# Laying out weights in advance, modulation by multiply-and-sum into columns, and a beginning by single chunks, in a decoder layer on one core

## The chip, the core and the metric

The kernel runs on one core of one Trainium2 chip. The metric is the device time of one execution in microseconds (us), lower is better. Engines are named as in the profile: PE does matmuls (PEld its weight loads), DVE is the vector engine, ACT the scalar engine, POOL the general one, and SP issues most of the transfers (DMAs). Each engine takes its instructions in the order of its own queue, and waits on semaphores for others.

## The reference

One layer of a decoder, 256 rows (SEQ) of width 2048 (D_MODEL), all in float32. A conditioning vector c gives six modulation vectors of 2048 each; the rest is a normalisation, a large input projection, three kinds of attention, an output projection and a SwiGLU FFN.

```python
mod = jax.nn.silu(c) @ w_ada[l] + b_ada[l]          # w_ada: 2048 x 12288
shift1, scale1, gate1, shift2, scale2, gate2 = jnp.split(mod[:, None, :], N_MOD, axis=-1)
h = rms_norm(x, norm1_gain[l]) * (1 + scale1) + shift1
x = x + gate1 * mixing_sublayer(h, w_in[l], ...)    # w_in: 2048 x 13840
h = rms_norm(x, norm2_gain[l]) * (1 + scale2) + shift2
x = x + gate2 * swiglu(h, w_ffn_in[l], w_ffn_out[l])   # D_FF = 5632
```

Of the 13840 columns of w_in, 16 (from column 7680) are a low-rank gate; the others are taken in blocks of 512.

## The kernel before

**Products.** x is kept turned, features on partitions: `xT` and the modulated `hT` are 16 chunks (k) of 128 features by 256 rows. A product of a block of 512 weight columns is done in three matmuls for each chunk and each of two row tiles (`mm3`, L173 to L176): high by high, low by high, high by low, with each float32 operand split into a high and a low half. The high half of a weight tile is cast by ACT (L166, or L244 in pairs), the low half subtracted by DVE (L167, or L230). `load_weights` brings two chunks of 512 columns a transfer, through SP, into a ring "raw" of 4 tiles. `block` (L178) runs the chunks of a block and calls `tick`, which lets so many steps of background work run per pair of chunks. Where two blocks are done together (`fast_products` and `load_pair`, L217), products of sums and differences of blocks save one in eight; these are the gate columns of the projection, FFN units from 2 on, and the output.

**Order.** The first projection goes through groups of chunks, `GROUPS` = (0,3), (3,7), (7,11), (11,16), so that the product of the first chunks can begin while the modulation of the later ones is still computed. For each group, all 13 first blocks of columns are multiplied by the group's chunks, and the sums stay in slots A0 to A12. A scheduler sorts the instructions by priority and by their order in the program; `prio` raises a stretch of the program by a number of steps, and `issue_after` ties an instruction behind another.

**Modulation.** w_ada is read in rows (k on partitions), and `ada_mac` (L426, L432) multiplies a piece of it by silu(c) of that chunk (`csil`, one value per partition) and adds it to an accumulator of as many columns: 16 pieces per accumulator. What is left then is a sum over the partitions. For columns, `turn_acc` has PE transpose the accumulator, 128 columns at a time (L481), and DVE sums the turned tile (L486, L1123); `finish_columns` adds the bias b_ada. For rows spread over all partitions (gate1, gate2), `rows_of` and `rows_of_gate2` multiply the accumulator's halves by a matrix of ones on PE (L1144, L1145, L1620). The first group's accumulator is built from 16 pieces of 128x768 before any product; norm1 is computed from x in rows, which PE turns with a diagonal matrix; `keep_warm` (L590) issues matmuls without use in PE's idle time. The accumulator of shift1 and scale1 lives in slot "ada", and so, in turn, does that of shift2 and of scale2. 24 of the 32 pieces of gate2 are taken in the output projection w_out and FFN units 0 and 1, the other 8 in the output stage (`gate2_end`).

**FFN.** Units 0 and 1 of 11 are done one block at a time, gate columns, then up columns; DVE multiplies the two (L1555). Before unit 2 the program drains all background work (`flush`). From unit 2 on, `load_pair` loads into a ring of the 4 "raw" tiles and `MORE_RAWS`: slot "AR1" until unit 10 and slot "ada" until unit 9. Unit 2's first load goes to "ada".

```python
    MORE_RAWS = (("AR1", 10), ("ada", 9))
    state["raws"] = state["tiles"] = 0
    for i in range(NFF):
        if i == FAST[0]:
            flush()
        state["more_rooms"], state["more_raws"] = rooms_until(i, MORE_ROOMS), rooms_until(i, MORE_RAWS)
```

## Time and profile before

| what | value |
|---|---|
| median of 3 runs | 1574.76 us (1573.27 to 1574.9) |
| profiled execution's span | 1573.4 us, 20259 instructions |
| matmuls of L174, L175, L176 into acc from whi, wlo and H | 998 each, mean 390 to 393 ns |
| low halves of single loads, L167 on DVE | 277, 323.0 us |
| multiply-and-adds of 128x1024 into "ada" from ring AR, L432 on DVE | 39, 49.8 us, mean 1282 ns |
| DMA | 402.26 MB, mean 256 GB/s |

The span is that of one execution taken by the profiler, and stands 1.4 us below the median of the timed runs. A matmul's duration in the trace overlaps its neighbours', so its cost on PE is read from the distance of two starts. The rows of a timeline are: start, duration, engine, line, operation, output <- inputs, shapes, count, and in brackets the idle time before it with what ended it. A name such as `ada<-w_ffn_in` means a transfer or an instruction that writes the tile in slot "ada" from w_ffn_in.

### The profile page before, as it was taken

The page shows a single profiled execution, that of the slowest core. Times are in us where ns is not written, and L with a number is a line of the kernel's source. Part 1 is how long each engine was busy: PE and PEld are TensorE (multiplying, and loading weights), DVE is VectorE, ACT ScalarE, POOL GpSimd, SP SyncE. Part 2 cuts the span into 40 slices and gives each one's busy share as a digit, 9 for nine tenths or more (in the row PEclk, how much of TensorE's full clock was granted, in tenths as well). Part 3 has the DMA queues.
Part 4 walks back from the last instruction along what each step waited for, and adds up shares of the span by engine and source line. Part 5 has one row for each costly group of instructions (what it writes and reads, how often), then busy time and mean ns, then how long its engine had stood idle before and what let it go on. Part 6 is the DMA issues. An engine that isn't in the chain of part 4 may idle for free.

```text
span 1573.4 us, 20259 instructions
## 1 busy us (share of the span) xinstructions
PE 1563.8 (99%) x7180; PEld 1294.6 (82%) x7180; DVE 1404.4 (89%) x1722; ACT 879.7 (56%) x1220; POOL 12.4 (1%) x24
## 2 busy tenths in 40 slices
PE   9999999999999999999999999999999999999998
PEld 7878888888888888888888888888888888888887
DVE  6889996898898999987987889999999999899996
ACT  5654448875765555444444645556555555455553
POOL 1000000000000000000000000000000000000000
PEclk9999999999999999999999999999999999999999
DMA  9999997677797877989997896665666567876664
GB/s 333 355 326 319 335 316 232 217 223 227 238 320 261 275 258 238 314 278 324 313 331 263 298 310 218 191 210 189 202 210 203 174 200 236 289 229 201 222 213 135
DMA packets 196317, 402.26 MB, mean 256 GB/s; under 512 B 13102, under 2 KB 28116, under 8 KB 196216
## 3 DMA queue, kind: packets, MB, share of 16 engines
q1 hardware_dynamic: 194952, 397.75, 76.4%
q0 software_dynamic: 1088, 3.16, 0.5%
q8 instruction: 56, 0.92, 0.2%
q14 instruction: 45, 0.37, 0.1%
q10 hardware_dynamic: 176, 0.07, 0.0%
HBM read 395.68 MB, written 5.24 MB: 255 GB/s over the span
## 4 chain that ended last, share of the span: by engine, by line
PE 94%; ACT 2%; DVE 2%; DMA 1%; issue 1%; ACTq 0%; DVEq 0%
PE acc L176 21%; PE acc L174 21%; PE acc L175 21%; PE misc L176 8%; PE misc L174 8%; PE misc L175 8%; PE acc L590 1%; PE misc L959 1%; ACT whi L166 1%; PE misc L1310 1%; DVE wlo L167 0%; PE misc L583 0%; DMA AR<-w_ada 0%; PE misc L481 0%; DMA raw<-w_in 0%
## 5 line engine op out<-in xcount | busy, mean ns | idle before, releaser
L166 ACT CAST whi<-raw 128x1024 fp32r<-128x1024 f32 (+1 forms) x277 | 278.9, 1012 | 285.9 <-PE acc L176 174.7
L167 DVE TENSOR_TENSOR wlo<-raw,whi 128x1024 fp32r<-128x1024 f32 (+1 forms) x277 | 323.0, 1176 | 98.0 <-ACT whi L166 96.9
L174 PE MATMUL acc<-whi,H 128*128 128x512 f32 x998 | 390.9, 393 | 0.9 <-ACT H L602 0.8
L175 PE MATMUL acc<-wlo,H 128*128 128x512 f32 x998 | 389.7, 390 | 0.7 <-DVE wlo L167 0.7
L176 PE MATMUL acc<-whi,H 128*128 128x512 f32 x998 | 389.7, 391 | 0.5 <-DVE H L609 0.4
L176 PEld LDWEIGHTS acc<-whi,H 128*128 128x128 f32 x998 | 187.6, 188 | 40.9 <-DVE H L609 1.7
L174 PEld LDWEIGHTS acc<-whi,H 128*128 128x128 f32 x998 | 187.7, 188 | 39.2 <-ACT H L602 1.0
L175 PEld LDWEIGHTS acc<-wlo,H 128*128 128x128 f32 x998 | 187.8, 188 | 38.8 <-DVE wlo L167 1.1
L244 ACT CAST whi<-raw 128x1024 fp32r<-128x1024 f32 (+1 forms) x126 | 121.0, 973 | 69.0 <-PE acc L176 28.4
L230 DVE TENSOR_TENSOR wlo<-raw,whi 128x1024 fp32r<-128x1024 f32 (+1 forms) x126 | 139.9, 1124 | 12.8 <-ACT whi L244 11.5
L176 PE MATMUL acc<-whi,A 128*128 128x512 f32 x221 | 86.0, 389 | 0.0
L174 PE MATMUL acc<-whi,A 128*128 128x512 f32 x210 | 82.0, 390 | 0.0
L175 PE MATMUL acc<-wlo,A 128*128 128x512 f32 x210 | 81.7, 389 | 0.0
L174 PE MATMUL misc<-whi,H 128*128 128x512 f32 (+1 forms) x185 | 71.6, 387 | 0.0
L176 PE MATMUL misc<-whi,H 128*128 128x512 f32 (+1 forms) x185 | 71.6, 387 | 0.0
L175 PE MATMUL misc<-wlo,H 128*128 128x512 f32 (+1 forms) x185 | 71.5, 387 | 0.0
L230 DVE TENSOR_TENSOR A<-raw,A 128x1024 fp32r<-128x1024 f32 (+2 forms) x58 | 55.6, 964 | 0.5
L432 DVE SCALAR_TENSOR_TENSOR ada<-AR,csil,ada 128x1024 f32<-128x1024 f32 x39 | 49.8, 1282 | 4.2 <-DMA AR<-w_ada 4.2
L176 PEld LDWEIGHTS acc<-whi,A 128*128 128x128 f32 x221 | 41.5, 188 | 8.7
L244 ACT CAST A<-raw 128x1024 fp32r<-128x1024 f32 (+1 forms) x35 | 34.5, 991 | 25.0 <-PE acc L176 14.8
L244 ACT CAST whi<-A 128x1024 fp32r<-128x1024 f32 x26 | 27.4, 1056 | 36.0 <-DVE A L230 28.1
L175 PEld LDWEIGHTS acc<-wlo,A 128*128 128x128 f32 x210 | 39.4, 188 | 8.1
(710 smaller groups left out, 3078.3 us busy)
## 6 DMA issues: line engine op xcount, KB each, us to landing
raw<-w_in SPq DMA_DIRECT2D x190, 512.0 KB, 4.9
raw<-w_ffn_in SPq DMA_DIRECT2D x135, 512.0 KB, 4.7
raw<-w_ffn_out SPq DMA_DIRECT2D x73, 512.0 KB, 5.0
AR<-w_ada SPq DMA_DIRECT2D x61, 512.0 KB, 4.6
raw<-w_out SPq DMA_DIRECT2D x32, 512.0 KB, 5.9
OS<-w_ada SPq DMA_DIRECT2D x24, 512.0 KB, 5.9
AR<-w_ffn_in SPq DMA_DIRECT2D x22, 512.0 KB, 4.3
KD<-w_ada SPq DMA_DIRECT2D x21, 512.0 KB, 5.1
```

The source lines that it names most:

```text
L166: state["cast"] = nc.scalar.copy(hi[:, :n, :], raw[:, :n, :])
L167: state["split"] = nc.vector.tensor_tensor(lo[:, :n, :], raw[:, :n, :], hi[:, :n, :].bitcast(F32), op=ALU.subtract)
L174: nc.tensor.matmul(ps, lh, rh, start=start, stop=False, skip_group_check=seeded)
L175: nc.tensor.matmul(ps, lh, rl, start=False, stop=False, skip_group_check=seeded)
L176: state["mm"] = nc.tensor.matmul(ps, ll, rh, start=False, stop=stop, skip_group_check=seeded)
L230: done = nc.vector.tensor_tensor(dst, x, y, op=ALU.subtract)
L244: nc.scalar.copy(hi[:, :n, :], src)
L432: nc.vector.scalar_tensor_tensor(acc, raw, c, acc, op0=ALU.mult, op1=ALU.add)
L590: state["warm"] = nc.tensor.matmul(ps, ones_r, wide, start=True, stop=True)
L959: nc.tensor.matmul(ps[:n, t * N_GLA + h, :].rearrange("p (s l) -> p s l", l=L), at(f, h, t)[:, :n], odd(at(f, h, t)), start=True, stop=True,)
L1310: nc.tensor.transpose(ps[:, i, :], src[:, i * P : (i + 1) * P], ident)
```

## The change

**Layout in numpy.** Every weight matrix is laid out as blocks [column block, 128 partitions, chunk, 512], so that a load of two chunks reads 4 KB in one piece per partition instead of two rows of 2 KB. x comes turned (`x_t`) and in blocks (`x_blocks`), w_ada turned (`ada_t`), all small vectors with c and b_ada as columns of one array (`k_vec`), the 16 gate columns of w_in alone (`w_a`). The loads and turns of vectors go.

**Modulation.** silu(c) is spread once over all partitions, as a row of 2048, in `cB`, which takes slot "ada" and stays there. With w_ada turned, a piece is 128 modulation outputs on partitions by 1024 inputs; `column_mac` multiplies it by half of cB and sums along the row in one instruction, into one column. Two give an output column of 128, the bias being the start value. So there are 192 of them: 64 for shift1 and scale1, 32 each for shift2, gate1, scale2 and gate2. The transposes and sums on PE and DVE go. Rows (silu(c) itself, gate1, gate2) are made by `spread`: halves, one transpose, 16 matmuls of 128x128 with a broadcast column of `pick`, and four copies.

**Beginning.** `first_chunks` takes the first four blocks of columns by single chunks (0, 1, 2) into all eight PSUM banks; norm1 is a multiplication of turned x by a spread root (`normed`); h is made chunk by chunk behind its modulation (`ada_chunks`), not at the end of a group.

**gate2.** All 32 of its pieces are taken in w_out and FFN units 0 and 1, with rates 0.9 and 0.7 there; `gate2_end` goes.

```diff
+    cB = S("ada", [P, D])
+    def column_mac(v, seg, j, half, raw):
+        o = BADA + seg * KC + j
+        part = v[:, 0, j : j + 1]
+        return nc.vector.tensor_tensor_reduce(
+            out=raw, in0=raw, in1=cB[:, half * HALF : (half + 1) * HALF], scale=1.0,
+            scalar=part if half else vec[:, o : o + 1], op0=ALU.mult, op1=ALU.add,
+            accum_out=v[:, 1, j : j + 1] if half else part,
+        )
...
+    def spread(v, quarters, tag, first=False):
+        t = S(tag, [P, 2, P], F32R)
+        hl, vT = t[:, 0, :], t[:, 1, :]
+        nc.vector.memset(hl.bitcast(F32), 0.0)
+        nc.vector.tensor_copy(hl[:, :KC], v)
+        nc.vector.tensor_tensor(hl[:, KC : 2 * KC], v, hl[:, :KC].bitcast(F32), op=ALU.subtract)
...
+            nc.tensor.transpose(ps, hl.bitcast(F32), ident)
+        nc.scalar.copy(vT, ps)
...
+                    state["spread"] = nc.tensor.matmul(
+                        ps[:, j * P : (j + 1) * P], pick[:, k : k + 1].to_broadcast([P, P]), vT, start=True, stop=True
+                    )
+            (nc.vector.tensor_copy if first else nc.scalar.copy)(dst, ps)
...
+    def ada_chunks(k0, k1):
+        for k in range(k0, k1):
+            if k % 4 == 0:
+                normed(state["root"], k, k + 4)
+            for seg in (SEG_SCALE1, SEG_SHIFT1):
+                for half in range(2):
+                    with prio():
+                        raw = S(ADA_TAGS[count % len(ADA_TAGS)], [P, HALF])
+                        load_column(raw, seg, k, half)
...
+                            column_mac(mod1[seg], seg, k, half, raw)
+                    if half and seg == SEG_SHIFT1:
+                        make_h(k)
+                    yield
...
+        for k in range(k1):
+            if k:
+                with tc.issue_after(state["h_lo"].ins):
+                    chunk_macs(k, rows[4 * k : 4 * k + 4])
...
+            for i, b in enumerate(ahead):
+                for t in range(NT):
+                    mm3(pss[i][t], *h_at(k, t), *parts[k][i], k == 0, k == k1 - 1)
...
-RATES_OP, RATES_FFN, RATE_OUT = (0.85, 0.5, 0.0), (0.75, 0.9, 0.7, 0.6), 0.5
+RATES_OP, RATES_FFN = (0.9, 0.7, 0.0), (0.75, 0.9, 0.7, 0.6)
...
-WARM = (22, 38, 13)
+WARM = (5, 4, 3, 3, 3, 18)
...
     def gate2_bg():
-        acc = biased([S(tag, [P, 2 * NB]) for tag in ("OS0", "T3")], SEG_GATE2)
-        yield from ada_segment_steps(acc, SEG_GATE2, None, False, range(GATE2_CUT))
+        yield from ada_segment_steps(gate2_v, SEG_GATE2, None)
         yield from last_macs()
-    def gate2_end():
...
-                state["load"] = nc.sync.dma_start(
-                    raw[:, :n, :],
-                    src[ka * P : (ka + n) * P, c0 : c0 + w].rearrange("(k p) c -> p k c", p=P),
-                )
+                state["load"] = nc.sync.dma_start(raw[:, :n, :], src[b, :, ka : ka + n, :])
...
-    gate_pair(1, GATE_PAIRS_3, misc_bank, acc_bank, (("A9", "A10"), ("X1", "T0"), ("ada",)), ("X2", "A8"))
+    gate_pair(1, GATE_PAIRS_3, misc_bank, acc_bank, (("A9", "A10"), ("X1", "T0"), ("T4", "T5")), ("X2", "A8"))
...
-        xs = S("ada", [P, D])
+        xs = []
+        for tag in ("OS0", "T3"):
+            xs += [x for x in S(tag, [P, 2, NB]).rearrange("p a c -> a p c")]
```

**What stands in the queues.** Rows give the line, the operation, the output and its inputs with their tile numbers, and the shape.

DVE at the beginning, before: the last full multiply-and-adds into the accumulator of group 0, then the last piece in quarters, the bias, and h (H is a half of h).

```order
L432 SCALAR_TENSOR_TENSOR ada_329<-OS_39_166,csil,ada_329 128x768
L432 SCALAR_TENSOR_TENSOR ada_329<-OD_168,csil,ada_329 128x768
L432 SCALAR_TENSOR_TENSOR ada_329<-A_41_170,csil,ada_329 128x2x128 x3
L492 TENSOR_TENSOR mod_101<-misc_348,bada 128x1 x2
L492 TENSOR_TENSOR mod_101<-misc_358,bada 128x1 x2
L495 SCALAR_TENSOR_TENSOR mod_101<-mod_101,vec 128x1 x2
L606 TENSOR_SCALAR scr_354<-T_6_102,mod_101 128x256
```

The same place in the changed kernel, DVE, chunk 1: an ISA row of 128x1024 is a multiply-and-sum, the ISA row of 128x1 behind it reads its sum; L639 is a low half of two blocks' weights.

```order
L423 ISA T_19_111,scale_92<-T_19_111,ada_90,vec 128x1024
L423 ISA scale_92 128x1
L423 ISA A_21_113,shift_91<-A_21_113,ada_90,vec 128x1024
L423 ISA shift_91 128x1
L423 ISA T_20_112,scale_92<-T_20_112,ada_90,scale_92 128x1024
L423 ISA scale_92 128x1
L423 ISA A_22_114,shift_91<-A_22_114,ada_90,shift_91 128x1024
L423 ISA shift_91 128x1
L431 SCALAR_TENSOR_TENSOR scale_92<-scale_92,vec 128x1
L639 TENSOR_TENSOR wlo_312<-raw_136,whi_311 128x1024
L564 TENSOR_SCALAR scr_307<-T_2_93,scale_92,shift_91 128x256
```

Sixteen multiply-and-adds ahead of the first h have become four multiply-and-sums ahead of each chunk's.

DVE between FFN unit 1 and unit 2, before: L1555 are unit 1's products of gate and up; A_1870 is a part of unit 2's pairs, from a tile in "ada".

```order
L1555 TENSOR_TENSOR scr_8394<-scr_8394,acc_8398 128x512
L1555 TENSOR_TENSOR scr_8396<-scr_8396,acc_8399 128x512
L230 TENSOR_TENSOR X_1866_8600<-KD_8586,X_1865_8599 128x1024
L230 TENSOR_TENSOR wlo_8596<-OD_8585,whi_8595 128x1024
L432 SCALAR_TENSOR_TENSOR T_1561_7147<-A_1812_8330,csil,T_1561_7147 128x1024
L230 TENSOR_TENSOR A_1870_8608<-ada_8603,A_1869_8607 128x1024
```

In the changed kernel, DVE at the same place (L1484 are the products, ada_90 is cB, L228 is L230 before):

```order
L1484 TENSOR_TENSOR scr_8135<-scr_8135,acc_8139 128x512
L1484 TENSOR_TENSOR scr_8137<-scr_8137,acc_8140 128x512
L423 ISA KC_8067,gate_6786<-KC_8067,ada_90,gate_6786 128x1024
L423 ISA gate_6786 128x1
L228 TENSOR_TENSOR wlo_8349<-OD_8338,whi_8348 128x1024
...
L423 ISA KD_8232,gate_6786<-KD_8232,ada_90,vec 128x1024
L423 ISA gate_6786 128x1
L228 TENSOR_TENSOR KD_8339<-AR_1795_8332,OD_8338 128x512
L423 ISA KC_8259,gate_6786<-KC_8259,ada_90,gate_6786 128x1024
L423 ISA gate_6786 128x1
```

Seven multiply-and-sums of gate2 stand behind the products (four of them in the rows left out), the last of them the last reader of cB in slot "ada".

SP, before, amid the loads of unit 1 (raw, L152): the first load of unit 2 into "ada".

```order
L152 DMA raw_8072<-w_ffn_in 128x2x512
L531 DMA T_1773_8103<-w_ada 128x1024
L224 DMA ada_8553<-w_ffn_in 128x2x512
L152 DMA raw_8078<-w_ffn_in 128x2x512
```

SP, changed: the load into "ada" stands behind the last load of w_ada's gate2 columns.

```order
L416 DMA KD_8232<-ada_t 128x1024
L416 DMA KC_8259<-ada_t 128x1024
L222 DMA AR_1825_8396<-w_ffn_in 128x1024
L222 DMA ada_8306<-w_ffn_in 128x1024
L222 DMA raw_8394<-w_ffn_in 128x1024
```

PE, changed, at the same place: acc_8140 is the up block of unit 1, misc_8458 the first product of unit 2, A_1783 the high half of the tile in "ada".

```order
L172 MATMUL acc_8140<-whi_8185,H_1600_7365 128x512
L173 MATMUL acc_8140<-wlo_8186,H_1600_7365 128x512
L174 MATMUL acc_8140<-whi_8185,H_1604_7369 128x512
L172 MATMUL misc_8458<-A_1783_8308,H_1597_7362 128x512
L172 MATMUL misc_8459<-A_1783_8308,H_1597_7362 128x512
```

The load of unit 2's first pair has moved from the middle of unit 1's loads to behind gate2's last ones, and unit 2's first product, which needs that pair, follows unit 1's last matmul directly on PE.

More of the change, by code (lines that the diff above doesn't have):

```diff
@@ L39 @@
 AHEAD = 4000
[L40 to L41 removed]
+WARM = (5, 4, 3, 3, 3, 18)
+FIRST = 4
+BADA = 58
 GROUPS = ((0, 3), (3, 7), (7, 11), (11, 16))
@@ L473, in column_sum @@
-    def column_sum(ps, acc):
-        return nc.tensor.matmul(ps, acc, ones[:, 0:1], start=True, stop=True)
-    def turn_acc(acc, behind=None):
-        ps = misc_bank([P, acc.shape[1] // P, P])
-        for i in range(acc.shape[1] // P):
-            with tc.issue_after(behind) if behind is not None else nullcontext():
-                nc.tensor.transpose(ps[:, i, :], acc[:, i * P : (i + 1) * P], ident)
-        return ps
-    def turned_sums(dst, acc, behind=None):
-        nc.vector.reduce_sum(dst, turn_acc(acc, behind), axis=AX.X)
@@ new lines, in squares, with root_of @@
+    def squares(j, sums):
+        sq = S(("X1", "X2", "AR0", "AR1")[j], [P, 4, T])
+        nc.scalar.activation(sq, xT[j], AF.Square)
+        for n in (2, 1):
+            nc.vector.tensor_tensor(sq[:, :n], sq[:, :n], sq[:, n : 2 * n], op=ALU.add)
+        return nc.tensor.matmul(sums, ones, sq[:, 0, :], start=j == 0, stop=j == 3)
+    def root_of(sums):
+        act = nc.scalar.activation
+        v, y, z, r = (x for x in S("X0", [P, 4, T]).rearrange("p a t -> a p t"))
+        act(v, sums, AF.Identity, bias=eps_c[:, 0:1], scale=1.0 / D)
@@ L1129, in rows_of, with columns @@
[L1129 to L1147 removed]
+    def columns(seg, v):
+        if seg == SEG_SCALE2:
+            scaled_gain(v, ROW_N2, 0, KC)
+        mod2[seg] = v[:, 1, :]
+        yield
@@ L1148, in rows_of @@
+    def rows_of(name, v, tags):
+        rows = [S(tag, [P, 2 * NB]) for tag in tags]
+        quarters = [a[:, c : c + NB] for a in rows for c in (0, NB)]
+        yield from spread(v[:, 1, :], quarters, {"gate1": "T6", "gate2": "X0"}[name])
         state[name] = quarters
-    def halves(acc):
-        return [acc[:, : 2 * NB], acc[:, 2 * NB :]]
     def background():
         for seg in (SEG_SHIFT2, SEG_GATE1, SEG_SCALE2):
-            if seg == SEG_GATE1:
-                acc = biased([S(f"T{4 + j}", [P, 2 * NB]) for j in range(2)], seg)
-                yield from ada_segment_steps(acc, seg, rows_of("gate1", seg, acc), False)
-            else:
-                acc = S("ada", [P, D])
-                yield from ada_segment_steps(halves(acc), seg, columns(seg, acc))
+            v = columns_of(f"mod_{seg}")
+            done = rows_of("gate1", v, ("T4", "T5")) if seg == SEG_GATE1 else columns(seg, v)
+            yield from ada_segment_steps(v, seg, done)
@@ L1602, in trunk, with gate2_steps @@
     hooks = {at: (lambda n=n: sums_of_unit(n)) for n, at in enumerate((2, 4, 6))}
[L1603 to L1625 removed]
+    state["rate"] = 0.0
+    gate2_rows = rows_of("gate2", gate2_v, ("A2", "A3"))
+    def gate2_steps(n):
+        for _ in range(n):
+            next(gate2_rows, None)
     for n in range(2):
```

525 lines of the change are left out of this document (206 added, 319 removed).

## The prediction

> **What bounds the kernel now.** I read the page's busy times first, then its chain of work that ended last, then busy times by stretch.
>
> ```profile
> PE 1563.8 (99%) x7180; PEld 1294.6 (82%) x7180; DVE 1404.4 (89%) x1722; ACT 879.7 (56%) x1220; POOL 12.4 (1%) x24
> PE 94%; ACT 2%; DVE 2%; DMA 1%; issue 1%; ACTq 0%; DVEq 0%
> 0.00:32.00 32.00, 29.08 (x150) 24.22 (x150) 19.63 (x36) 15.52 (x35) 4.26 (x13) 1.00 0.96 340
> 32.00:84.00 52.00, 51.69 (x224) 42.46 (x224) 42.86 (x51) 32.15 (x51) 0.00 (x0) 0.97 1.00 350
> 84.00:157.00 73.00, 71.88 (x319) 58.91 (x319) 68.97 (x81) 36.32 (x44) 0.00 (x0) 1.00 0.92 318
> 157.00:239.00 82.00, 82.00 (x368) 67.61 (x367) 79.46 (x108) 38.76 (x47) 0.00 (x0) 1.00 0.95 321
> 951.00:976.00 25.00, 25.00 (x116) 20.77 (x115) 24.47 (x29) 13.14 (x16) 1.06 (x2) 1.00 0.60 202
> 957.52 0.39 PE L176 MATMUL acc<-whi,H 128*128 128x512 f32 x1
> 957.75 0.39 PE L174 MATMUL misc<-A,H 128*128 128x512 f32 x1
> ```
>
> PE is busy 99% and is 94% of the chain, so a matmul taken away is worth its pace. The stretch rows give length, then PE, PEld, DVE, ACT and POOL, the granted clock, the DMA share and GB/s. In the stretch that holds FFN units 1 and 2 (the fifth), PE is busy for all 25.00 us, at one 512-column matmul per 957.75 − 957.52 = 0.23 us; and the step to unit 2 is that pair of rows, with no gap. But DVE stands at 24.47 of 25.00 there and at 79.46 of 82.00 in group 2 of the projection: it is a near second, and whatever the change makes DVE or its buffers do late, PE feels.
>
> **The change, part by part.** The sum is made against this execution's span, 1573.4 us; the median of the runs is 1574.76, so 1.4 is added at the end.
>
> *PE work.*
>
> ```profile
> 82.34 1.04 PE L481 MATMUL misc<-ident,ada 128*128 128x128 f32 x8
> 83.14 0.47 PE L174 MATMUL acc<-whi,H 128*128 128x512 f32 x1
> 682.29 0.28 PE L1144 MATMUL misc<-T,ones_r 128*128 128x256 f32 x1
> 682.53 0.40 PE L174 MATMUL acc<-whi,A 128*128 128x512 f32 x1
> 1442.09 0.39 PE L1620 MATMUL misc<-AR,ones_r 128*128 128x512 f32 x1
> 1442.32 0.39 PE L1620 MATMUL misc<-A,ones_r 128*128 128x512 f32 x1
> 307.32 0.22 PE L850 MATMUL misc<-T,ones_r 128*128 128x128 f32 x1
> 307.38 0.40 PE L849 MATMUL misc<-T,T 128*128 128x384 f32 x1
> ```
>
> Eight transposes of L481 hold PE from 82.34 to 83.14, 0.10 each; 50 go after the beginning: −5.0. The gate1 rows go: 8 pairs of 256 columns at 682.53 − 682.29 = 0.24 a pair, −1.9. The gate2 rows go: 8 at 0.23, −1.85. `spread` brings 2 × 16 matmuls of 128 columns and 2 transposes. One of 128 columns with a plain operand takes 307.38 − 307.32 = 0.06; a broadcast stationary operand is not in the trace, so 0.06 to 0.10 (the transpose's pace), and I take 0.08: +2.6, with the transposes +0.2. Net **−6.0** (−7 to −5). The 512-column products stay at 6,378.
>
> *The price d of one reduce.* The change has 192 multiply-and-reduce instructions of 128x1024, each followed by a 128x1 accumulator read. Neither is in the trace. Nearest rows:
>
> ```profile
> 953.75 1.28 DVE L432 SCALAR_TENSOR_TENSOR OS<-A,csil,OS 128x1024 f32<-128x1024 f32 x1
> 954.94 1.22 DVE L230 TENSOR_TENSOR wlo<-raw,whi 128x1024 fp32r<-128x1024 f32 x1
> 956.08 0.69 DVE L230 TENSOR_TENSOR KD<-AR,OD 128x512 f32<-128x512 f32 x1
> 956.68 0.69 DVE L230 TENSOR_TENSOR wlo<-AR,whi 128x512 fp32r<-128x512 f32 x1
> 0.80 0.06 DVE L342 MEMSET eps_c<- 128x1 f32 x1 [0.80 <-PEq L1678]
> 11.44 0.18 ACT L560 ACTIVATION_READ_ACCUMULATOR H<-A 128x1 f32 x1
> ```
>
> By starts, the multiply-and-add occupies DVE for 1.19, the subtraction of the same size 1.14, one of half the size 0.60. The read lies between 0.06 (a 128x1 memset) and 0.18 (ACT's read). So d is 1.14 + 0.06 = 1.20 to 1.28 + 0.18 = 1.46; I take 1.28, the multiply-and-add's start-to-start plus a short read.
>
> [...]
>
> *The beginning.*
>
> ```profile
> 14.71 1.06 ACT L560 ACTIVATE H<-A 128x1024 f32<-128x1024 f32 x1 [0.23 <-DMA A<-x]
> 32.31 0.65 PE L174 MATMUL acc<-whi,H 128*128 128x512 f32 x1 [0.80 <-ACT H L602]
> 32.76 0.63 PE L175 MATMUL acc<-wlo,H 128*128 128x512 f32 x1
> 35.75 0.47 PE L176 MATMUL acc<-whi,H 128*128 128x512 f32 x1
> 32.33 0.88 DVE L609 TENSOR_TENSOR H<-scr,H 128x256 fp32r<-128x256 f32 x2
> 84.13 0.73 PE L174 MATMUL acc<-whi,H 128*128 128x512 f32 x2
> 85.53 0.50 PE L175 MATMUL acc<-wlo,H 128*128 128x512 f32 x1 [0.67 <-DVE wlo L167]
> 92.12 0.72 PE L176 MATMUL acc<-whi,H 128*128 128x512 f32 x2 [0.40 <-DVE H L609]
> ```
>
> Before, the first product starts at 32.31, after loads of about 3.7 MB that had landed when the last x part was read (14.71) and 16 multiply-and-adds. Afterwards, what chunk 0 needs is about as many bytes (vectors, x, its first three modulation pieces), four reduces and one h: 14.7 + 4 × 1.28 + 0.6 puts the first product near 20.5 (two low halves of h at 32.33 take 0.88). Those 12 us are not all kept, since DVE then paces the stage. A chunk of four blocks costs DVE 4 × 1.28 + 2 × 1.14 + 0.6 = 8.0 and PE 24 × 0.23 = 5.5. DVE ends chunk 2 at about 40.7 (three chunks of 8.0 from 16.7); the nine other blocks need 9 × (1.14 + 0.60) of splits, beside them 16 reduces at 1.28 for group 1, and about 4.7 of normalisation and h: 40.8, to 81.5. PE ends group 0 near 87.3, with the last blocks' matmuls behind their splits. Before, group 1 begins at 84.13 and waits to 85.53, say 85.1 of useful time. **+2** (−1.6 with d at 1.20 to +6 at 1.46). The wait for H near 92 goes with the group-end making of h: **−0.7**. Groups 1 and 2 give DVE 36 reduces in place of 32 multiply-and-adds in pieces; the 97% busy stretch has little room, I put **+1** (0 to 4).
>
> *gate2 and FFN unit 2: the deciding term.* The spread silu(c) sits in slot "ada" until gate2's last reduce. The FFN's first fast unit, unit 2, takes its first weight pair into that same slot. Before, the slot is free there, and the load is issued amid unit 1's loads. Afterwards, the load waits for the last gate2 reduce; seven reduces stand in DVE's queue behind unit 1's products (L1555 before), which wait for PE's last matmul of unit 1. And PE's next matmul needs the cast of that pair. Nothing else stands in PE's queue between them. So PE is idle for the whole chain:
>
> ```profile
> 957.88 1.28 DVE L1555 TENSOR_TENSOR scr<-scr,acc 128x512 f32<-128x512 f32 x2
> 959.09 1.23 DVE L230 TENSOR_TENSOR X<-KD,X 128x1024 fp32r<-128x1024 f32 x1
> ada<-w_ffn_in SPq DMA_DIRECT2D x19, 512.0 KB, 5.3
> gate<-T POOLq DMA_DIRECT2D x1, 512.0 KB, 2.9
> T<-w_ada SPq DMA_DIRECT2D x15, 512.0 KB, 6.7
> L244 ACT CAST A<-ada 128x1024 fp32r<-128x1024 f32 x6 | 6.3, 1051 | 0.7 <-PE misc L176 0.7
> ```
>
> Two products 959.09 − 957.88 = 1.21; seven reduces 8.96; the split and the half-size subtraction that stand among them 1.14 + 0.60; issue to landing 5.3 (the group's median; transfers of this size elsewhere take 2.9 to 6.7); the cast 1.05. Together 11.9 + 5.3 + 1.05 = **18.3** (15.3 with d at 1.20 and the shortest transfer, 20.9 with 1.46 and the longest). The transfer has no neighbours to hide behind: the wait is SP's, and the weights queued behind it on SP are late too, by the same time, not more. After a stop PE may come back slow, as at 32.31, where eight matmuls to 35.75 took 0.43 each: 8 × 0.20 = **+1.6** (0 to 2.9). The gap here is far longer than the 0.80 us wait ahead of that row.
>
> The slots of other tiles that change hands (distances, gate rooms, norm2's rows) keep their sizes, and the warm-up matmuls run while PE waits for the first product: nothing for both, unless a slot's last reader is late, which would show as a wait like the one above.
>
> gate2 itself moves 8 multiply-and-adds from the output stage into w_out and units 0 and 1; PE has no wait on DVE of size in either stage that this would lift, so I put it at nothing. The relayout in numpy leaves bytes and the size of each load as they are.
>
> ```profile
> L166 ACT CAST whi<-raw 128x1024 fp32r<-128x1024 f32 (+1 forms) x277 | 278.9, 1012 | 285.9 <-PE acc L176 174.7
> ```
>
> The casts that read the loads are idle 285.9 us, and 174.7 of it ends with a matmul that frees a buffer, not with a transfer: PE's need for loads is covered, and faster ones are worth nothing where that holds. With the cover gone each load would cost up to its 5 us.
>
> Sum: −6.0 + 2 − 0.7 + 1 + 18.3 + 1.6 = +16.2: a span of 1589.6, a run of **1591**.
>
> **The rivals.** *A, faster.* The load into "ada" is not held: the reduces finish, and the pair lands and is cast, before PE's last matmul of unit 1. Then −6.0 + 2 − 0.7 + 1 = −3.7: 1571. It decides from the point at which the seven reduces stand ahead of unit 1's products on DVE. Against it: their place in the queue, which is fixed by program order. For it: DVE runs ahead of PE elsewhere. If moreover the beginning keeps its 12 us (reduces far cheaper than any row), 1563. Chance 0.09. *B, much slower.* [...] Chance 0.05. *C, no change.* The chain is half hidden (say four reduces already done, a short transfer and a quick clock, 10 us less) and the beginning 4 better: +2, 1577. Chance 0.04.
>
> **How the numbers follow.** Forecast 0.82. All low ends: −7 − 1.6 − 0.7 + 0 + 15.3 + 0 = +6.0, a run of 1581. All high ends: −5 + 6 − 0.7 + 4 + 20.9 + 2.9 = +28.1, 1603. The range 1580 to 1604 holds the forecast and leaves out A, B and C, 0.18. A measurement can tell about 0.2%, 3.1 us, from no change. Faster by more is A (0.09), within it C (0.04), slower the forecast and B (0.87).
>
> **What would show it.** One PE gap of 15 to 21 us between unit 1's last and unit 2's first matmul, released by ACT's cast from "ada", behind a transfer issued right after the last reduce. First product near 20.5; group 0 ended near 87. Rows of L481, L1144 and L1620 gone. A reduce and its read at 1.20 to 1.46 by starts. What would make it wrong: the reduces before the products on DVE, a price far from 1.28, or PE gaps in groups 1 and 2 that DVE's lead does not cover.

## The result, and the profile after

The changed kernel takes 1607.98 us (median of 4 runs, 1606.77 to 1610.35) against 1574.01 us of the kernel before, measured beside it: a ratio of 1.0218, with an interval of 1.0206 to 1.0231. It is 34 us slower. The prediction was 17 us slower, 1591, in a range of 1580 to 1604: the direction and the largest single cause were right, the sum was half of what came.

The page of the changed kernel, the lines that answer to those shown of before:

```profile
span 1608.6 us, 19949 instructions
PE 1556.9 (97%) x7043; PEld 1283.5 (80%) x7043; DVE 1406.2 (87%) x1889; ACT 866.1 (54%) x1185; POOL 4.0 (0%) x11
PE 75%; DVE 10%; DMA 7%; ACT 4%; issue 4%; SPq 0%; DVEq 0%; ACTq 0%
```

PE is busy for 6.9 us less than before (1563.8) and the span is 35 us longer, so PE stands idle for 42 us more. (A part of the busy time that is gone is warm-up: 36 such matmuls in place of 73.) The chain that ended last was PE for 94%, and DVE, DMA and ACT had 5% of it; now these hold 21%, since the chain leaves PE at each long wait and follows a queue back.

The same stretches as before, and the one with the change from FFN unit 1 to unit 2 (columns as before: length, PE, PEld, DVE, ACT, POOL, granted clock, DMA share, GB/s):

```profile
0.00:32.00 32.00, 22.51 (x85) 17.85 (x85) 23.84 (x51) 11.99 (x16) 0.69 (x6) 1.00 0.96 362
32.00:84.00 52.00, 44.94 (x174) 33.89 (x175) 48.23 (x77) 28.59 (x46) 0.00 (x0) 0.93 0.86 299
84.00:157.00 73.00, 73.00 (x321) 59.78 (x320) 67.84 (x93) 37.74 (x45) 0.00 (x0) 1.00 0.93 332
157.00:239.00 82.00, 80.49 (x355) 66.33 (x354) 78.24 (x112) 36.70 (x42) 0.00 (x0) 1.00 0.92 324
960.00:1000.00 40.00, 20.52 (x81) 16.02 (x80) 29.15 (x40) 10.51 (x12) 0.00 (x0) 0.70 0.53 178
```

In the last row PE is busy for half of the time and stands at 0.70 of its clock. In the second PE is busy for 7 us less than before in the same stretch, while DVE has gone from 42.86 to 48.23.

Where PE stands still shows in its timeline: in brackets the idle time and what ended it.

```profile
33.06 1.65 PE L172 MATMUL acc<-whi,H 128*128 128x512 f32 x3 [2.97 <-ACT H L560]
...
68.76 0.73 PE L172 MATMUL acc<-whi,H 128*128 128x512 f32 x2 [0.94 <-ACT whi L164]
70.02 0.50 PE L173 MATMUL acc<-wlo,H 128*128 128x512 f32 x1 [0.52 <-DVE wlo L165]
...
220.12 0.50 PE L173 MATMUL acc<-wlo,H 128*128 128x512 f32 x1 [1.51 <-DVE wlo L165]
...
415.72 0.69 PE L777 MATMUL misc<-ident,A 128*128 128x128 f32 x2 [2.81 <-DVE A L765]
...
586.03 0.50 PE L172 MATMUL acc<-whi,H 128*128 128x512 f32 x1 [1.56 <-ACT whi L242]
587.36 0.50 PE L173 MATMUL acc<-wlo,H 128*128 128x512 f32 x1 [0.83 <-DVE wlo L228]
...
670.61 0.30 PE L367 MATMUL misc<-ident,T 128*128 128x128 f32 x1 [2.24 <-DVE T L359]
...
780.85 0.50 PE L173 MATMUL acc<-wlo,A 128*128 128x512 f32 x1 [1.13 <-DVE wlo L165]
...
988.76 1.22 PE L172 MATMUL misc<-A,H 128*128 128x512 f32 x2 [19.43 <-ACT A L242]
```

The matmuls of `mm3` are 6378 in both kernels (24 of them of 256 columns, the others of 512). Apart from the first four blocks they come in the same order but for a few, so the start of the n-th in one trace can be set beside the n-th of the other. The difference, worked out in this way, is the lag of the changed kernel; it is that of one execution each, and that of the changed kernel was the slowest of its four (1610.35):

| product | where | lag, us |
|---|---|---|
| 0 | first product | −7.9 |
| 100 | in group 0 | +0.9 |
| 260 | group 1 | +2.8 |
| 860 | end of group 2 | +2.5 |
| 1180 | first blocks of the last group | +0.1 |
| 1500 | after the wait at 415 us | +6.4 |
| 2140 | after the waits at 587 us | +8.1 |
| 2500 | after the wait at 670 us | +13.2 |
| 3700 | end of FFN unit 1 | +11.4 |
| 3740 | in unit 2 | +34.4 |
| 6377 | last | +35.1 |

So of 35 us, 23 come at unit 2, 9 between products 860 and 3700, and about 3 in the beginning. In seven small steps of 0.5 to 0.9 us, 5.4 together, the lag shrinks where the transposes of L481 are gone.

The wait at unit 2, by the queues of DVE, SP and ACT:

```profile
970.94 1.28 DVE L1484 TENSOR_TENSOR scr<-scr,acc 128x512 f32<-128x512 f32 x2
972.13 1.28 DVE L423 CUSTOM_DVE_ANT_0 KC<-KC,ada,gate 128x1024 f32<-128x1024 f32 x1
...
979.30 1.28 DVE L423 CUSTOM_DVE_ANT_0 KD<-KD,ada,vec 128x1024 f32<-128x1024 f32 x1
...
981.23 1.28 DVE L423 CUSTOM_DVE_ANT_0 KC<-KC,ada,gate 128x1024 f32<-128x1024 f32 x1
982.54 0.33 SPq L222 DMA_DIRECT2D ada<-w_ffn_in  x1
987.66 1.04 ACT L242 CAST A<-ada 128x1024 fp32r<-128x1024 f32 x1 [3.46 <-DMA ada<-w_ffn_in]
```

Products, seven reduces, issue of the load, landing, cast, and at 988.76 PE: the chain is the one that the prediction described, link by link.

The price of one reduce, from two that follow each other:

```profile
214.50 1.28 DVE L423 CUSTOM_DVE_ANT_0 OD<-OD,ada,scale 128x1024 f32<-128x1024 f32 x1
215.71 0.09 DVE L423 DVE_READ_ACCUMULATOR2_ANT scale<- 128x1 f32 x1
215.71 1.28 DVE L423 CUSTOM_DVE_ANT_0 T<-T,ada,vec 128x1024 f32<-128x1024 f32 x1
```

215.71 − 214.50 = 1.21 us from start to start; the read of the sum (0.09) starts together with the next reduce, and from there to the next start, at 216.91, it is 1.20 us, so the read costs nothing beside the reduces.

### The profile page after: what moved, and what is told of

It reads as the page before. It is cut to its first block, busy times and chain, and to the rows that moved or that the text cites. A ratio compares the mean times of both kernels' runs of the same rounds, so it can differ in the third digit from the quotient of the medians.

```text
span 1608.6 us, 19949 instructions
## 1 busy us (share of the span) xinstructions
PE 1556.9 (97%) x7043; PEld 1283.5 (80%) x7043; DVE 1406.2 (87%) x1889; ACT 866.1 (54%) x1185; POOL 4.0 (0%) x11
## 4 chain that ended last, share of the span: by engine, by line
PE 75%; DVE 10%; DMA 7%; ACT 4%; issue 4%; SPq 0%; DVEq 0%; ACTq 0%
PE acc L173 17%; PE acc L174 17%; PE acc L172 17%; PE misc L172 7%; PE misc L173 7%; PE misc L174 7%; DMA raw<-w_in 2%; DVE wlo L165 2%; DVE wlo L228 2%; ACT whi L164 1%; DVE A L228 1%; DMA AR<-ada_t 1%; DMA raw<-w_br_gla 1%; PE misc L930 1%; DMA KD<-ada_t 1%
## 5 line engine op out<-in xcount | busy, mean ns | idle before, releaser
L164 ACT CAST whi<-raw 128x1024 fp32r<-128x1024 f32 (+1 forms) x269 | 272.1, 1017 | 277.8 <-PE acc L174 124.0
L172 PE MATMUL acc<-whi,H 128*128 128x512 f32 x986 | 386.5, 394 | 9.8 <-ACT H L560 4.9
L165 DVE TENSOR_TENSOR wlo<-raw,whi 128x1024 fp32r<-128x1024 f32 (+1 forms) x269 | 314.3, 1177 | 89.5 <-ACT whi L164 88.3
L174 PE MATMUL acc<-whi,H 128*128 128x512 f32 x986 | 384.5, 391 | 0.1
L228 DVE TENSOR_TENSOR wlo<-raw,whi 128x1024 fp32r<-128x1024 f32 (+1 forms) x126 | 139.7, 1122 | 18.2 <-ACT whi L242 16.8
L242 ACT CAST whi<-raw 128x1024 fp32r<-128x1024 f32 (+1 forms) x126 | 121.0, 973 | 63.2 <-PE acc L174 26.9
L174 PE MATMUL misc<-whi,H 128*128 128x512 f32 (+1 forms) x197 | 76.2, 387 | 0.0
L173 PE MATMUL misc<-wlo,H 128*128 128x512 f32 (+1 forms) x197 | 76.2, 387 | 0.0
L172 PE MATMUL misc<-whi,H 128*128 128x512 f32 (+1 forms) x197 | 76.2, 387 | 0.0
L228 DVE TENSOR_TENSOR A<-raw,A 128x1024 fp32r<-128x1024 f32 (+2 forms) x58 | 55.4, 961 | 3.6 <-ACT A L242 3.2
L242 ACT CAST A<-raw 128x1024 fp32r<-128x1024 f32 (+1 forms) x35 | 34.4, 990 | 31.7 <-PE acc L174 8.7
L172 PE MATMUL misc<-A,H 128*128 128x512 f32 x73 | 29.8, 411 | 19.4 <-ACT A L242 19.4
L423 DVE CUSTOM_DVE_ANT_0 AR<-AR,ada,vec 128x1024 f32<-128x1024 f32 x30 | 38.4, 1278 | 9.8 <-DMA AR<-ada_t 9.8
```

The source lines that it names most:

```text
L164: state["cast"] = nc.scalar.copy(hi[:, :n, :], raw[:, :n, :])
L165: state["split"] = nc.vector.tensor_tensor(lo[:, :n, :], raw[:, :n, :], hi[:, :n, :].bitcast(F32), op=ALU.subtract)
L172: nc.tensor.matmul(ps, lh, rh, start=start, stop=False, skip_group_check=seeded)
L173: nc.tensor.matmul(ps, lh, rl, start=False, stop=False, skip_group_check=seeded)
L174: state["mm"] = nc.tensor.matmul(ps, ll, rh, start=False, stop=stop, skip_group_check=seeded)
L228: done = nc.vector.tensor_tensor(dst, x, y, op=ALU.subtract)
```

## The experiments

Times are medians beside runs of the kernel before on the same chip; the ratio is to that, with its interval. "The changed kernel" is at 1608.0, ratio 1.0218.

**1. The wait at unit 2: the slot, or DVE's load?** Three edits, each taking the wait away by another means. First (run no_slot), no load into "ada" for unit 2 alone:

```diff
-        state["more_raws"] = rooms_until(i, MORE_RAWS)
+        state["more_raws"] = rooms_until(i, MORE_RAWS)[: 1 if i == 2 else 2]
```

> The changed kernel, except that unit 2 alone doesn't load into slot "ada" (the pairs of unit 2 take AR1 and the four raw tiles). Theory T (the slot holds the load, and the load holds PE): the gap of 19.8 us between unit 1's last and unit 2's first matmul falls to under 3 us, the slow matmuls after it (3 us) go, and the time falls from 1608 by 16 to 23 us, to 1585 to 1592. Rival Q (the queue: PE waits for DVE, which has seven reduces to do before unit 2's low halves, whatever slot the load takes): the gap stays at 8 to 12 us, released by DVE, and the time is 1597 to 1601.

Measured 1599.57, 1.0165 (1.0149 to 1.018). The wait is gone, and the lag at product 3740 is 9.7 instead of 34.4. But at product 4100 it is 26.1: PE waits in units 2 to 4, again and again, for casts and low halves.

```profile
986.57 0.50 PE L172 MATMUL acc<-X,AR 128*128 128x512 f32 x1 [1.72 <-ACT X L242]
...
1007.80 0.72 PE L172 MATMUL acc<-whi,OS 128*128 128x512 f32 x2 [1.19 <-ACT whi L242]
...
1036.84 0.50 PE L172 MATMUL acc<-whi,H 128*128 128x512 f32 x1 [1.02 <-ACT whi L242]
```

T was right on what the wait is, and wrong on what it costs: 16 of the 23 us come back. The cast behind the first of these waits had itself been idle for 10.74 us until DVE was done with a sum of unit 2's weights, which stands behind gate2's reduces; DVE is busy for 37.72 of the 39 us there:

```profile
985.47 1.04 ACT L242 CAST X<-KD 128x1024 fp32r<-128x1024 f32 x1 [10.74 <-DVE KD L228]
966.00:1005.00 39.00, 35.34 (x156) 27.86 (x155) 37.72 (x53) 15.56 (x18) 0.00 (x0) 1.00 0.59 197
```

So the queue of rival Q is real, and shows once the slot is out of the way. Second (early_gate2), gate2's steps earlier, so that the last reduce stands ahead of unit 1's products:

```diff
-RATES_OP, RATES_FFN = (0.9, 0.7, 0.0), (0.75, 0.9, 0.7, 0.6)
+RATES_OP, RATES_FFN = (1.2, 0.9, 0.0), (0.9, 1.1, 1.0, 0.0)
```

> The changed kernel with other rates for gate2's steps: w_out 1.2, 0.9 and FFN units 0 and 1 at 0.9, 1.1, 1.0, 0, so that the last gate2 reduce stands ahead of unit 1's products in DVE's queue; slot "ada" is used as before. Both T and Q: the gap at unit 2 goes (under 3 us). T and Q differ in nothing here; a third theory, that unit 2's weights come late for their bytes (DMA bound there), would keep a gap of 5 us or more. Time 1584 to 1592, unless the faster steps make DVE late in w_out or units 0 and 1, which would show as PE waits between 880 and 965 us.

Measured 1599.69, 1.017 (1.0153 to 1.0187). No wait at unit 2, but 13 us of lag come up between products 3060 and 3700 (6.6 to 19.3), in w_out and at norm2:

```profile
856.36 0.49 PE L172 MATMUL acc<-whi,A 128*128 128x512 f32 x1 [2.12 <-ACT whi L164]
858.41 0.79 PE L173 MATMUL acc<-wlo,A 128*128 128x512 f32 x1 [1.56 <-DVE wlo L165]
881.30 1.17 PE L1343 MATMUL misc<-ident,OS 128*128 128x128 f32 x8 [3.59 <-DVE OS L1334]
```

Two opposite repairs end at the same time, but not for the same reason. Here loads are late: the cast behind the first wait had been idle for 4.30 us until a load of w_out landed, and DVE's sum ahead of norm2 for 6.99 us until a load of x did, while DVE was busy for only 8.81 of the 16 us from 856 to 872 us.

```profile
854.32 1.04 ACT L164 CAST T<-raw 128x1024 fp32r<-128x1024 f32 x1 [4.30 <-DMA raw<-w_out]
870.85 0.69 DVE L1322 TENSOR_TENSOR A<-A,scr 128x512 f32<-128x512 f32 x1 [6.99 <-DMA A<-x_blocks]
```

Why these loads are late with the other rates isn't shown. Third (tail_out), the last 8 reduces back in the output stage:

```diff
+    state["cB"] = [cB[:, :HALF], cB[:, HALF:]]
...
+        yield from ada_segment_steps(gate2_v, SEG_GATE2, None, range(12))
...
+    def gate2_end():
+        state["cB"] = [S(tag, [P, HALF]) for tag in ("A2", "A3")]
+        for h in range(2):
+            with prio():
+                nc.sync.dma_start(state["cB"][h], cB_away[h])
+        yield from ada_segment_steps(gate2_v, SEG_GATE2, None, range(12, KC))
```

> The changed kernel, with the last 8 of gate2's 32 reduces back in the output stage, as before the change (silu(c) is put away to DRAM and brought back into A2 and A3 there); the rates of the changed kernel stay, so gate2's 24th reduce stands ahead of unit 1's products. Removing the wait for the slot alone gave 8 us of the 23 back, because waits of PE for DVE came up in units 2 to 4 instead. Theory B (a debt: DVE has no room for 8 more reduces of 1.2 us between w_out and unit 4, so the wait is only moved): with the 8 gone from there the whole 23 us are saved, no new waits in units 2 to 4, 1584 to 1587. Rival S (the slot's ring: a smaller ring of raw tiles made units 2 to 4 late in that run, not DVE's load): waits between 880 and 1060 us remain or the output stage becomes late by 5 us or more, 1590 to 1598.

Measured 1584.52, 1.0065 (1.005 to 1.008): 23.5 us saved, with no new waits in units 2 to 4 (lag 9.0 at product 3740, 9.0 at 4100) and none in the output stage (9.6 at the end). By the lag, the step at unit 2 falls from 23.0 to 2.2 us, so 21 of the 23.5 us come from there; the others are waits in the middle that were shorter in this profile (lag 6.8 at product 3700 instead of 11.4), which the edit doesn't touch. Theory B holds for unit 2 and what follows: the 8 reduces are 8 × 1.21 = 9.7 us of DVE's time, DVE has no room for them there, and in the output stage they cost nothing (+0.6 of lag from product 3740 to the end, +0.7 in the changed kernel, which has none there). (Their 8 loads move with them; that it is DVE's time rests on the rows of no_slot.) That DVE has no room in w_out either isn't shown (in early_gate2 it was loads), and rates that spread the steps otherwise over w_out and units 0 and 1 weren't tried.

**2. The beginning.** Fewer warm-up matmuls (warm):

```diff
-WARM = (5, 4, 3, 3, 3, 18)
+WARM = (5, 4, 0, 0, 0, 10)
```

> The changed kernel with fewer warm-up matmuls at the beginning (5, 4, 0, 0, 0, 10 for 5, 4, 3, 3, 3, 18). Theory: the warm-up matmuls between the four parts of the sum of squares hold up the root, so that the first product comes at 24.4 us instead of the 20.5 forecast; without them the root is done 3 to 4 us earlier, the first product comes at 20.5 to 21.5, and since DVE is without a break from there, the end of group 0 (92 us) and the whole come 2 to 4 us earlier: 1604 to 1606. Rival: the beginning waits for the last loads, first product and time as they are, 1607 to 1609.

Measured 1608.31, 1.0214 (1.0199 to 1.0229). The first product comes at 22.2 instead of 24.4, so the warm-up matmuls do hold the root up; but by product 200 the kernel is 2.9 us later than the changed one, and the time is the same. The first product's time isn't what counts. Next (tiny_first), DVE's work taken away: in `column_mac`, for chunks 3 to 15,

```diff
+        if seg in mod1 and j >= 3:
+            raw = raw[:, :4]
```

> The changed kernel, but the reduces of shift1 and scale1 for chunks 3 to 15 (52 of 192) take only the first 4 of each 1024 elements; it leaves out the rest of these sums. Loads and waits stay. Theory D of the prediction (DVE's work is the bound of group 0 from the first product on: 16 reduces of 1.2 us stand beside its nine later blocks): group 0 ends 5 us or more before 92 us, and time falls by as much. Rivals A and L (ACT's order, or loads): group 0 ends within 2 us of 92 us.

Measured 1607.03, 1.0196 (1.0176 to 1.0216). The rows from 22 us to 92 us, the changed kernel first, then this one:

```profile
22.00:50.00 28.00, 20.91 (x79) 15.11 (x77) 27.96 (x44) 12.81 (x20) 0.00 (x0) 0.93 0.89 310
50.00:92.00 42.00, 38.86 (x158) 30.18 (x159) 36.51 (x59) 25.34 (x42) 0.00 (x0) 0.96 0.91 323
```

```profile
22.00:50.00 28.00, 21.51 (x82) 15.57 (x81) 26.80 (x47) 11.99 (x19) 0.00 (x0) 0.94 0.89 309
50.00:92.00 42.00, 37.60 (x152) 29.05 (x152) 19.80 (x55) 25.65 (x41) 0.00 (x0) 0.96 0.92 319
```

With DVE's work from 50 to 92 us nearly halved, PE does no more. Until 50 us DVE is busy for 27.96 and 26.80 of the 28 us, so theory D can stand for the first three chunks, and it falls for the nine blocks after them. Then (early_loads), the loads of chunk 2 in free slots:

```diff
+            raw = raws[k, i] = S(("A5", "A6")[i // 2], [P, 2, NB]) if k == 2 else wp.tile(...)
```

> The changed kernel, but the weights of chunk 2 for the first four blocks are loaded into A5 and A6, free until then, with the loads of the third chunk's modulation, instead of into the raw ring, where SP's queue stood still until the splits of chunk 0. Theory L (loads are the bound of the beginning: with the reduces of group 1 cut to 4 elements DVE was busy 19.8 of 42 us from 50 to 92 us, and group 0 ended no earlier; the queue moved 281 GB/s from 30 to 60 us against 336 before the change): the hole in the transfers between 25 and 50 us shrinks, and group 0 ends 2 to 4 us earlier than 92 us, time 1603 to 1606. Rival: ACT's order (copies out of PSUM ahead of the casts, waits at 67 and 78 us) is the bound, nothing moves, 1607 to 1609.

Measured 1605.63, 1.0194 (1.0178 to 1.0209). The time lies within L's range, but the runs spread from 1601.94 to 1609.02, and in the trace, which is of the slowest of them, the transfers from 30 to 60 us were no denser (265 GB/s against 281), and the waits at 68 and 79 us stayed. L isn't borne out in this form. h at the group's end, written so in the program (group_h):

> The changed kernel, with h of a group made at the group's end again, not chunk by chunk. Theory A (ACT's order: h's two ACT instructions wait for a reduce, and the casts of the next weights stand behind them and behind the copies out of PSUM, which puts the waits of 2.3 us at 67 and 78 us and of 1.9 us at 218 us): these waits go, one or two of about 1 us come at the ends of groups (as before the change at 84 and 91 us), 1602 to 1605. Rival D (DVE's work is the bound of the beginning to 90 us, whatever ACT does): group 0 ends where it did, 1606 to 1610.

Measured 1606.53, 1.0206 (1.0191 to 1.0221). This run tells nothing on A: ACT's queue still had h chunk by chunk, since the scheduler takes what it thinks ready, and the waits were those of the changed kernel to 0.1 us. Tied behind a cast it moves (h_late):

```diff
+            if n == len(blocks) - 2:
+                held = state["cast"].ins
...
+        for k in range(k0, k1):
+            with tc.issue_after(held):
+                make_h(k)
```

> The changed kernel, with h of groups 1 to 3 tied on ACT behind the cast of the last block but one of the group before, so that no reduce stands ahead of a cast within the group (in the run with h written at the group's end the order of ACT's queue was still chunk by chunk, and the waits stayed to 0.1 us). Theory A (h's ACT instructions wait for reduces, and casts stand behind them): the waits of 2.3 us at 67 and 78 us and of 1.9 us at 218 us go, one or two of 1 us come at group ends, 1602 to 1605. Rival L (loads: group 0's end and the wait at 218 come from weights that land late, since in this kernel the casts wait for loads of w_in where they waited for PE): the waits stay or reappear at a cast that waits for its load, 1606 to 1609.

Measured 1605.34, 1.02 (1.0185 to 1.0216). The wait at 220 us is gone (its 1.8 us of lag with it): there, casts did stand behind h, which waited for a reduce. At 68 and 79 us the waits are unchanged. Last (casts_first), the copies out of PSUM behind the next casts:

```diff
+                        with tc.issue_after(state["cast"].ins):
+                            nc.scalar.copy(dst[:, t, :], pss[t])
```

> The changed kernel, with ACT's copies of a block of group 0 out of PSUM tied behind the casts of the next block's weights (in the trace the cast that PE waits for at 67 and 78 us stands behind a copy that waits for PE). Theory O (ACT's order of copies and casts): the waits at 67 and 78 us (1.1 and 0.7 us more than a matmul's pace each, 3.6 us together) go, and what follows is 3 to 4 us earlier at 105 us, 1603 to 1605. Rival L2 (the raw ring and its loads: early loads of chunk 2 alone changed nothing): they come back at the loads, 1606 to 1609.

Measured 1606.89, 1.0214 (1.0201 to 1.0227). The cast no longer waits behind a copy; now it waits behind h, on ACT:

```profile
73.16 0.60 ACT L560 ACTIVATE H<-T,shift,scale 128x256 fp32r<-128x256 f32 x1 [3.29 <-DVE shift L423]
73.67 1.55 ACT L164 CAST whi<-raw 128x1024 fp32r<-128x1024 f32 x2
```

So in the traces two things of ACT's queue hold the same casts, and each repair alone leaves the other. Both together weren't tried with group 0 included. The intervals of all six runs of this part overlap that of the changed kernel, so no run shows a gain in time here, and what the 3 us of the beginning are due to stays open.

**3. The waits in the middle: DVE's time, the order, or late loads?** The three additional yields in `spread` (slack):

```diff
-        yield
+        for _ in range(slack):
+            yield
```

> The changed kernel with three more steps of background between the halves of gate1 and their transpose in `spread`. Theory M1 (order: the waits in the middle come from small DVE work that stands behind reduces and splits in DVE's queue while its matmul already stands in PE's): the wait of 2.6 us at 668 us and the slow matmuls behind it (2 us) go, the others stay, time 1603 to 1605. Theory M2 (loads of the turned w_ada come late and hold DVE as a whole): the wait stays or moves to another matmul, time 1606 to 1609.

Measured 1602.92, 1.0189 (1.0173 to 1.0204): the wait at 670 us and its slow matmuls went, 4.6 us of lag between products 2460 and 2480, about as M1 has it. In the twelve profiles of the changed kernel and its variants without the slack this step is 0.5 to 5.3 us, in all six with it 0.0: the order causes it, and 4.6 us was a large draw. Contiguous pieces of w_ada (contig):

```diff
-        return nc.sync.dma_start(raw, I["ada_t"][o : o + P, half * HALF : (half + 1) * HALF])
+        return nc.sync.dma_start(raw, I["ada_t"][half, o : o + P, :])
```

> The changed kernel with the turned w_ada laid out so that each loaded piece of 128x1024 is 512 KB in one stretch, instead of 4 KB rows 8 KB apart. M2 (these loads land late for their layout: 5.4 us into AR against 4.6 before): landing falls to under 5 us, DVE's waits for them (17 us in all) shrink, and waits of PE in the middle go, time 1598 to 1604. M1: landing and time hardly change, 1606 to 1610.

Measured 1600.68, 1.0169 (1.0154 to 1.0185), with the issue row of the changed kernel ahead of this one's:

```profile
AR<-ada_t SPq DMA_DIRECT2D x61, 512.0 KB, 5.4
```

```profile
AR<-ada_t SPq DMA_DIRECT2D x61, 512.0 KB, 4.9
```

They land 0.5 us sooner, DVE's idle time that ends with such a load falls from 17.0 to 10.5 us in all (12.9 and 14.1 in slack and tail_out, which leave the layout as it is), and the time by 7 us, clear of the noise: late loads have a part in the waits, as M2 has it. And DVE's time taken away, for shift2, gate1 and scale2 (tiny):

```diff
+        if seg in (SEG_SHIFT2, SEG_GATE1, SEG_SCALE2):
+            raw = raw[:, :4]
```

> The changed kernel, but the reduces of shift2, gate1 and scale2 (96 of the 192, those of the middle) take only the first 4 of each 1024 elements; it leaves out the rest of these sums, so its output isn't the reference's. Every load, wait and order stays. Theory M1 (DVE's time for the reduces is what puts PE's waits at 412, 584, 668 and 779 us there): the four waits go but for what stands in `spread`, and the gain of the PE work taken away shows, 1588 to 1594. Theory M2 (DVE is held by the late loads of the turned w_ada, in order, whatever the reduces cost): waits stay, at the places where DVE waits for a load, 1598 to 1605. The wait at 218 and the one at unit 2 stay in both.

Measured 1599.92, 1.0157 (1.0137 to 1.0177). The waits at 415, 587 and 670 us are gone, and that at 780 us is 0.46 us; the lag at product 3060 is 2.3 instead of 11.6. The waits went as M1 has it, though DVE's idle time for loads of w_ada rose to 26.1 us. The time is above M1's range, and within M2's: the order of the stage from 320 to 430 us moved too (lag 5.8 at product 1180 instead of 0.1), so M1's gain didn't show in full. Taken together, it needs both: reduces of full length in DVE's queue, and loads that let them start late. That reading is argued from the two runs; which of the two a given wait is due to isn't settled, since the wait at 415 us also differed between profiles of kernels that are alike there (0.85 to 3.11 us).

**4. The layout alone** (relayout), on the kernel before:

```diff
-                    src[ka * P : (ka + n) * P, c0 : c0 + w].rearrange("(k p) c -> p k c", p=P),
+                    src[c0 // NB, :, ka : ka + n, :],
```

> The kernel before, with nothing changed but the layout of the seven weight matrices in DRAM (blocks, so that a load reads 4 KB in one piece per partition). Forecast of the prediction: worth nothing, 1573 to 1576, since the casts wait for PE and not for loads. Rival: fewer and longer pieces land earlier or disturb other loads less, 1568 to 1571; or later (the same bytes from fewer places), 1578 to 1582.

Measured 1575.17, 1.0007 (0.9998 to 1.0017). Worth nothing, as predicted.

**5. The repairs together.** Five versions (best1 to best5, in this order), each the changed kernel with the 8 reduces in the output stage, contiguous pieces and the slack, and more.

> The changed kernel with four repairs at once: the last 8 gate2 reduces in the output stage, w_ada's pieces in one stretch, the slack in the gate1 rows, the fewer warm-up matmuls. If the parts add (23 + 7 + 5 + 3 us), 1570, faster than the kernel before by 0.2%; if the waits in the middle are one debt that the parts share, 1575 to 1582.

> The changed kernel with the last 8 gate2 reduces in the output stage, w_ada's pieces in one stretch, the slack in the gate1 rows and h at the group's end; the warm-up as changed. If theory A holds, 1574 to 1578; if D, 1579 to 1582.

> The changed kernel with the last 8 gate2 reduces in the output stage, w_ada's pieces in one stretch, the slack in the gate1 rows, h late as above, and the transposes of the dilated q and k two and one chunks later in their block (for the wait at 412 us, where they stand on PE before DVE has the norms). If A holds and the wait at 412 us is one of order, 1570 to 1573, faster than the kernel before; if not, 1575 to 1579.

> As best3, with h late only for groups 2 and 3, the early loads of chunk 2, and the transposes of the dilated q and k three and two chunks later than in the changed kernel. If the early loads bring 2 to 4 us, 1571 to 1574, at or below the kernel before; if not, 1574 to 1576.

> As best3, with h late only for groups 2 and 3, and the copies of group 0 behind the next block's casts. If theory O holds, 1570 to 1573.5, at or below the kernel before; if L2, 1574.5 to 1578.

| version | time | ratio |
|---|---|---|
| best1 | 1582.43 | 1.0042 (1.0025 to 1.0059) |
| best2 | 1577.15 | 1.0021 (1.0011 to 1.0031) |
| best3 | 1576.71 | 1.0018 (1.0009 to 1.0027) |
| best4 | 1579.22 | 1.0032 (1.002 to 1.0043) |
| best5 | 1575.63 | 1.0018 (1.0009 to 1.0028) |

The single gains (23.5, 7, 5 us) don't add up: best2 is tail_out with contiguous pieces and slack (and with h written at the group's end, which moved nothing in group_h), and comes to 7 us less than tail_out, where the sum would be 12. In best5's trace, which is of its second fastest run, the middle is better than the kernel before (lag −3.0 at product 3060), the beginning is still +2.6 at product 260, and the end is at −1.0; but its runs spread from 1574.1 to 1580.97, and the median is above the kernel before. No version here beats it.

## Why the prediction was half right

**The direction and the deciding term.** Right: one wait at unit 2, between these two matmuls, for a load into "ada" held by the last gate2 reduce. It was put at 18.3, and 1.6 for the slow restart; it measured 19.43 of idle time and 3.3 of slow matmuls, 23.0 by the lag. The links were near: landing 5.04 (5.3 taken), cast 1.05, reduce 1.21 (1.28). Missing was that DVE comes late to the products: PE's last matmul of unit 1 starts at 968.9, the products at 970.94, behind low halves and a reduce that stood in the queue. This term was right in mechanism, and 3 us short.

**But it wasn't the price of the slot.** The prediction put gate2's move at nothing, beside the wait. The row of 24.47 of 25.00 us on DVE, which it quoted, left no room for reduces there. no_slot shows it: without the wait, 16 of its 23 us come back in units 2 to 4, behind DVE. With the 8 reduces moved out of the stage (tail_out), 21 of the 23 us are gone for good. So the wait was in large part the time in which DVE caught up, and the sum had the price of the move under the slot's name.

**The middle is the step that failed.** The prediction has "groups 1 and 2 … +1", which is near (the lag goes from +2.8 to +2.5 between products 260 and 860, where transposes of 1.8 us are gone), and then no term for waits up to unit 1, and no reason for having none. The price of a reduce, which the sum worked out, is right (1.21 against 1.19 of a multiply-and-add); what the reduces stand in front of in the queue, and when their loads land, isn't in it. From product 860 to 3700 the sum had −3.7 (32 transposes and the gate1 rows less, one `spread` more), and the lag grew by 8.9: that is 12.6 of the 19 us that the sum was short. The rest is 3 at unit 2, 1.5 in the beginning, and small differences in groups 1 and 2 and in the output stage. In the trace, PE is busy for 711.4 of the 721 us from 239 to 960 us, 8.3 less than before, and two stretches there at half clock (6.83 and 3.41 us) cost about 5 more, an estimate: half of their length. The runs point to three causes, since the waits shrink when each is taken away: reduces of full length in DVE's queue (tiny), loads of the turned w_ada that land 0.5 us later for their layout (contig), and `spread`, whose three small DVE instructions stand behind reduces while its transpose is already next on PE (slack, 4.6 us in this profile). The last took back more than leaving out gate1's matmuls was to gain, 1.9. The prediction took the casts to wait for PE and not for loads, by the group's row of before, 174.7 of 285.9 us; in the changed kernel that cover is thinner:

```profile
L164 ACT CAST whi<-raw 128x1024 fp32r<-128x1024 f32 (+1 forms) x269 | 272.1, 1017 | 277.8 <-PE acc L174 124.0
```

**The beginning** was +1.3 in the prediction (+2 and −0.7) and +2.8 at product 260, so near. Its parts were off in both directions, so that this is partly luck: the first product came at 24.4 and not 20.5 (2.2 of these 3.9 us go with fewer warm-up matmuls, by warm), and the nine blocks were not paced by DVE (tiny_first). What stands on ACT ahead of the casts is seen in the traces, but no run gained time by moving it.

**PE's savings.** The 5.0 of the transposes are in the trace, as the steps of the lag of 5.4 together. The output stage, where the sum had −0.5 (gate2's rows less, one `spread` more), shows +0.7. **Rival B**, much slower, is out: a reduce takes 1.21 us from start to start, near the 1.19 of the multiply-and-add, and no run shows one at twice that price.

Three slips in the working change next to nothing in the forecast: 1.19 and a read of 0.06 make 1.25, not 1.28; with its other terms rival A's second case comes to 1557, not 1563; and of the 6,378 products 24 have 256 columns.

## What to carry to other kernels

Where an engine is at 98% in a stage, as DVE was here with 24.47 of 25.00 us, look for the price of work moved into it in that stage, whatever wait seems to be the cause (without the wait, 16 of 23 us came back): take the wait away alone, see how much comes back, and move the work, not the wait. Two repairs with the same time can fail for different reasons (here DVE's work, and late loads), so follow each new wait back to what released it. When operations of the same price replace others, look at what stands behind each in the queues: a small instruction of a chain that PE waits for can cost as much as all that stands ahead of it (here 4.6 us, by the slack). An order written in the program isn't the order in the queue, so an experiment on order must be read in the queue first.
